# A decoder step in which the tail's memory pools wait for single tiles of the heads' memory

## The chip, the cores and the metric

The kernel runs on one core of a Trainium2 chip. The metric is device time in microseconds (us), from launch to the last output, as the median of several runs. The core has a matrix engine (PE), a vector engine (DVE), an activation engine (ACT), a general engine (POOL) that here mostly issues transfers, a sync engine (SP) that issues the other transfers, and 16 DMA engines that both issuers share. Each engine works through its own list of instructions in order; where one depends on another engine or on a transfer, it waits for a semaphore.

## The reference, cut to what matters

One inference step of one decoder layer on 512 prompt tokens and 8 sample tokens, in fp32. Two branches run side by side on the same normed input and are merged through gates; an MLP follows.

```python
h = _rmsnorm(x, norm1_g[l]) * (1.0 + sc1) + sh1
u = h @ w_in[l].astype(F32)
qa, fa, ia, oga, xb, yb, ga, gb = _split_cols(u)
...
o, S_new = _hgrn2(q, k, v, logf, st_hg[l])            # branch a: 8 heads, matrix state
o_a = (_rmsnorm(o, hg_onorm_g[l]) * jax.nn.silu(oga)).reshape(B, L, HG_HEADS * HG_DV)
...
hseq, h_last = _rglru(xc, r, ig, lru_lambda[l], st_lru[l])   # branch b: 1024 scalar recurrences
o_b = hseq * jax.nn.gelu(yb)

merged = (jax.nn.sigmoid(ga) * (o_a @ w_branch_a[l])
          + jax.nn.sigmoid(gb) * (o_b @ w_branch_b[l]))
x = x + g1 * (merged @ w_out[l])
h2 = _rmsnorm(x, norm2_g[l]) * (1.0 + sc2) + sh2
x = x + g2 * (jnp.square(jax.nn.relu(h2 @ w_ff1[l])) @ w_ff2[l])
```

## The kernel before

All activations stand transposed, 128 features by 520 tokens to a tile (512 prompt, 8 sample). A matrix product is made of three passes: each fp32 operand is split into a rounded part (`hi`) and the rest (`lo`), ACT makes the first (a cast) and DVE the second (a subtraction), and PE adds up hi·hi, hi·lo and lo·hi. One output block of 128 features takes 8 blocks of the input, each 6 matmuls (three products, two halves of 260 tokens), all at line 151. Weights come in by SP into `wst`, 512 KB at a time, and are split at lines 112 (ACT) and 115 (DVE).

The program has these stages. A start-up (to about 54 us in the profile) norms the input. Then `run` goes through the eight heads: `head` makes a head's columns, `rg_x`, `rg_y` and `rg_scans` make the blocks of branch b between them, and after every second head `heads_prompt` and `head_prompt` do the recurrence of two heads in levels (b = 1, 2, 4 ... 64: PE products of tile `X` at lines 664 to 673, then a DVE multiplication of `X` in place at line 680). Each finished block of branch b goes to DRAM (`obT_d`, line 856), each finished head too (`oaT_d`, line 749). Eight gate blocks follow (`gate`, line 175 is their sigmoid); behind the fourth of them stand `end_recurrences` and `begin_tail`.

`begin_tail` closes the pools of the heads and of branch b (`hg`, `rg`) and opens the tail's pools over the same memory: `tail` (five tiles `t` for loads), `ab` (sixteen tiles `a`: the split inputs of branch b, two to a block, and later the merged ones), `abb` (sixteen tiles `b`: the split inputs of branch a) and `misc`. `load_branches` then has POOL load the eight blocks of `obT_d` into `t` (line 882), each split into two `a` tiles by ACT (line 205) and DVE (line 206), and after them the eight of `oaT_d` (line 886, split into `b`). `load_xT` loads `xin` (line 929) on the same queue. The product with `w_branch_b` reads the `a` tiles block by block; between its matmuls stand small products of modulation rows (`mod_rows`, line 413), which read `wst` without a split.

A pool opened over memory that another pool has used makes its tiles wait for what was there. The pools `rg` and `hg` are opened with `reuse_waits="tile"`, so that a tile waits for the users of the very tiles it lies over. The tail's pools are opened without it: the first tile of each waits for everything that its pool's region held.

Instructions are put in order by a scheduler that runs a timing model over the whole program; `with self.urgent()` and `with self.together()` raise the priority of what stands under them. Each engine's order is then fixed.

Of the kernel before, what the change touches and what calls it, by code (L numbers as in the profile page):

```python
# [6 lines left out]
F32 = mybir.dt.float32  # L7
# [4 lines left out]
OP = mybir.AluOpType  # L12
# [6 lines left out]
T = L + NB  # L19
# [57 lines left out]
class Kernel:  # L77
# [383 lines left out]
    def norm_samples(self):  # L461
        nc = self.nc
        j = self.pmm.tile([128, 2, 512], F32, name="mm").rearrange("p a b -> p (a b)")
        nc.vector.tensor_tensor(j[:NB], self.xsn, self.xsn, OP.mult)
        nc.vector.tensor_reduce(self.ss1[:NB, NC:NC + 1], j[:NB], mybir.AxisListType.X, OP.add)

# [69 lines left out]
    def head_f(self, h, ps):  # L536

        nc = self.nc
        f = self.slot(self.ma, "ma")
        X = self.hg.tile([128, 3, T], F32, name="X", bufs=4)  # L540
        k = X[:, 1]
        with self.urgent():
            self.sigmoid(self.two(f), ps)
            self.sigmoid(self.two(k), ps, scale=-1.0)
        nc.vector.tensor_scalar(f, f, self.lb1[:, h:h + 1], self.lbf[:, h:h + 1], OP.mult, OP.add)
        nc.vector.tensor_scalar(k, k, self.lb1[:, h:h + 1], None, OP.mult)
        return f, X

# [7 lines left out]
    def head(self, h, first=None):  # L556
        nc = self.nc
        kf, kq, kv, kg = ([x] for x in self.head_cols(h))
        st = self.head_load(h)
        f, X = self.head_f(h, first[0] if first else self.gemm(kf, self.h)[:, :, :HALF])  # L560
        q = self.head_q(X[:, 2], first[1] if first else self.gemm(kq, self.h)[:, :, :HALF])
        og = self.slot(self.hg, "e")
# [22 lines left out]
        fkq = self.fkq[h % 4]  # L585
        for j, t in enumerate((f, X[:, 1], q)):
            nc.vector.tensor_copy(fkq[:, j, :NB], t[:, L:])  # L587
# [48 lines left out]
    def heads_prompt(self, hs):  # L636
        nc = self.nc
        two = [self.opened[h] for h in hs]
        tbs = [x[0][:, :L] for x in two]
        Xs = [x[1] for x in two]  # L640
        Ts = [self.hg.tile([128, 508], F32, name="tb", bufs=2) for _ in hs]
        to = 0
        a32 = self.hg.tile([128, 2, NC, 32], F32, name="a32", bufs=1)
        at = self.at

        def view(t, first_q, first_k, step, n, b):

            return bass.AP(tensor=t.tensor, offset=t.offset + first_q,
                           ap=[t.ap[0], [T + first_k - first_q, 2], [step, n], [1, b]])

        heads = lambda m, *shape: m[:, None].to_broadcast([128, 2, *shape])
        b = 1
        while b < C:
            n = L // (2 * b)
            p = self.pps.tile([128, 512], F32, name="ps")
            with self.together():
                for e, X in enumerate(Xs):
                    Q, K = X[:, 0], X[:, 1]
                    for c in range(NC):
                        if b == 1:  # L660
                            for j in range(4):
                                s, o = c * C + 32 * j, 256 * e + 64 * c
                                o = p[32 * j:32 * j + 32, o:o + 64].rearrange("p (x t) -> p x t", x=2)
                                nc.tensor.matmul(o, K[:, s:s + 32], X[:, 0::2, s:s + 32], start=True, stop=True)
                        elif b <= 32:
                            for j in range(0, 128, 32 if b < 32 else 64):
                                s, o = c * C + j, 128 * e + 32 * c
                                d = s if b < 32 else s + 32
                                nc.tensor.matmul(p[j:j + 32, o:o + 32], K[:, s:s + 32], Q[:, d:d + 32], start=True,
                                                 stop=True)  # L670
                        else:
                            s, o = c * C, 256 * e + 64 * c
                            nc.tensor.matmul(p[:64, o:o + 64], K[:, s:s + 64], Q[:, s + 64:s + 128], start=True,
                                             stop=True)
                if b == 64:
                    po = self.heads_sample(hs)
            for X, tb in zip(Xs, tbs):
                half = view(X, b, 0, 2 * b, n, b)
                fac = bass.AP(tensor=tb.tensor, offset=tb.offset, ap=[tb.ap[0], [1, 2], [2, n], [0, b]])
                nc.vector.tensor_tensor(half, half, fac, OP.mult)  # L680
            if b == 1:
                first = p.rearrange("p (e c x t) -> p e c x t", e=2, c=NC, x=2)
                nc.vector.tensor_tensor(a32, first[:, :, :, 1], heads(self.mdiag, NC, 32), OP.mult)
                p = first[:, :, :, 0]
            if b <= 16:
                p = p if b == 1 else p[:, :256].rearrange("p (e c t) -> p e c t", e=2, c=NC)
                nc.vector.copy_predicated(a32, heads(self.masks[b], NC, 32), p)
            elif b == 32:
                for j in (0, 64):
                    nc.scalar.copy(at[j:j + 32, :, :, j + 32:j + 64],  # L690
                                   p[j:j + 32, :256].rearrange("p (e c t) -> p e c t", e=2, c=NC))
            else:
                nc.scalar.copy(at[:64, :, :, 64:], p[:64].rearrange("p (e c t) -> p e c t", e=2, c=NC))
            for e, tb in enumerate(tbs):
                t2 = tb.rearrange("p (n two) -> p n two", two=2)
                tbs[e] = Ts[e][:, to:to + n]
                nc.vector.tensor_tensor(tbs[e], t2[:, :, 0], t2[:, :, 1], OP.mult)
            to += n
            b *= 2
        for j in range(0, 128, 32):  # L700
            nc.vector.tensor_copy(at[j:j + 32, :, :, j:j + 32], a32[j:j + 32])
        for e, h in enumerate(hs):
            self.head_prompt(h, tbs[e], at[:, e])
        self.heads_sample_done(hs, po)
# [929 lines left out]
    def begin(self):  # L1634
# [3 lines left out]
        nc = self.nc = InOrder(self.tc)  # L1638
# [162 lines left out]
        nc = plain  # L1801
        self.rgp = self.open_pool("rg", 2, reuse_waits="tile")
        self.hg = self.scope.enter_context(self.tc.tile_pool(name="hg", bufs=2, reuse_waits="tile"))
        self.opened = {}
        self.fkq = [self.hg.tile([128, 3, 32], F32, name=f"fkq{n}", bufs=1) for n in range(4)]
        self.at = self.hg.tile([128, 2, NC, C], F32, name="at", bufs=1)
        for t in (*self.fkq, self.at):
# [19 lines left out]
    def begin_tail(self):  # L1827
        self.close_pool()
        tc = self.tc
        self.misc = self.ctx.enter_context(tc.tile_pool(name="misc", bufs=1, side="right"))  # L1830
        self.right = ExitStack()
        self.abb = self.right.enter_context(tc.tile_pool(name="abb", bufs=16, side="right"))
        self.tail = self.open_pool("tail", 2)
        self.ab = self.scope.enter_context(tc.tile_pool(name="ab", bufs=16))
        self.load_branches()

    def begin_strassen(self):
# [36 lines left out]
```

## Time and profile before

| what | value |
|---|---|
| median of 3 runs | 1029.59 us (1029.26 to 1031.78) |
| profiled execution: its time | 1029.2 us |
| profiled execution: span from first to last instruction | 1027.4 us |
| PE busy | 997.1 us, 97% of the span |
| DVE, ACT, POOL busy | 677.3, 514.0, 123.8 us |
| mean clock granted to PE | 0.997 of full speed |

The span is 1.8 us shorter than that execution's time. PE sets the pace: what can be gained or lost is the time in which PE stands still, or is made to, so a wait of another engine counts only if PE ends up waiting for it. In the rows of the profile, "[2.02 <-ACT a L205]" behind an instruction says that its engine was idle 2.02 us before it, and that the idle time ended with ACT's instruction of line 205 that writes tile `a`. A matmul of plain fp32 operands counts twice (x8 are four instructions).

### The profile page before, as it was taken

What the parts mean: (1) busy time and instruction counts of PE and PEld (TensorE: products, weight loads), DVE (VectorE), ACT (ScalarE), POOL (GpSimd) and SP (SyncE); (2) the same over time, 40 slices, a digit from 0 to 9 for tenths busy, and PEclk for the clock granted to TensorE, in tenths of its full rate; (3) what the DMA queues carried; (4) which work ended last, traced back from release to release, by engine and by line L of the source; (5) the groups of instructions that cost most, each with busy time, mean ns of one, the idle gap of its engine ahead of it and who ended that gap; (6) DMA issues with size and microseconds to landing.
All of it is one profiled execution on the core that took longest, in us unless ns stands there. A gap on an engine that the chain in (4) does not pass through costs nothing. (4 is left out here: it accounts for less than half of the span.)

```text
span 1027.4 us, 23569 instructions
## 1 busy us (share of the span) xinstructions
PE 997.1 (97%) x9756; PEld 965.4 (94%) x9756; DVE 677.3 (66%) x1428; ACT 514.0 (50%) x964; POOL 123.8 (12%) x229
## 2 busy tenths in 40 slices
PE   4999999999999999989999999999999999999997
PEld 2899899999999999969999999999999999999997
DVE  6785868687596867355233347677776776777685
ACT  4555644644574563342122235466556655656663
POOL 3210000000000001011000001011321231232150
PEclk9999999999999999999999999999999999999999
DMA  9673353444334435268555568322672484274242
GB/s 324 218 206 110 98 157 103 136 130 133 101 105 147 116 115 166 90 230 265 165 162 167 164 182 242 91 83 63 134 183 74 93 181 118 52 160 98 63 83 84
DMA packets 201822, 143.67 MB, mean 140 GB/s; under 512 B 6767, under 2 KB 189703, under 8 KB 201707
## 3 DMA queue, kind: packets, MB, share of 16 engines
q1 hardware_dynamic: 191090, 128.08, 41.7%
q0 software_dynamic: 10608, 14.05, 6.9%
q8 instruction: 76, 1.25, 0.5%
q14 instruction: 32, 0.25, 0.1%
q10 hardware_dynamic: 16, 0.03, 0.0%
HBM read 123.61 MB, written 11.26 MB: 131 GB/s over the span
## 5 line engine op out<-in xcount | busy, mean ns | idle before, releaser
L151 PE MATMUL mm<-h,whi 128*128 128x260 f32 (+1 forms) x2944 | 489.5, 285 | 0.1
L151 PEld LDWEIGHTS mm<-h,whi 128*128 128x128 f32 x2944 | 409.1, 188 | 4.5 <-ACT whi L112 3.3
L151 PE MATMUL mm<-h,wlo 128*128 128x260 f32 x1472 | 301.9, 284 | 0.0
L115 DVE TENSOR_TENSOR wlo<-wst,whi 128x1024 fp32r<-128x1024 f32 x164 | 200.0, 1221 | 121.5 <-ACT whi L112 120.4
L112 ACT CAST whi<-wst 128x1024 fp32r<-128x1024 f32 x164 | 171.9, 1049 | 206.7 <-PE mm L151 178.8
L151 PEld LDWEIGHTS mm<-h,wlo 128*128 128x128 f32 x1472 | 230.1, 189 | 0.6 <-issue 0.4
L151 PE MATMUL mm<-a,whi 128*128 128x260 f32 x512 | 84.3, 285 | 2.0 <-ACT a L205 2.0
L151 PEld LDWEIGHTS mm<-a,whi 128*128 128x128 f32 x512 | 70.4, 188 | 4.6 <-ACT a L205 2.5
L151 PE MATMUL mm<-a,wlo 128*128 128x260 f32 x256 | 52.3, 284 | 0.0
L882 POOL DMA_DIRECT2D t<-obT_d x8 | 4.4, 550 | 384.5 <-PE ps L623 343.1
L1275 DVE TENSOR_TENSOR f<-f 128x260 f32<-128x260 f32 x64 | 27.3, 427 | 27.6 <-ACT f L1270 26.9
L1264 ACT ACTIVATE ft<-ft,fsh 128x512 f32<-128x512 f32 (+2 forms) x36 | 24.0, 675 | 36.1 <-DVE ft L1261 36.1
L151 PE MATMUL mm<-b,whi 128*128 128x260 f32 x256 | 41.1, 282 | 0.0
L1267 POOL TENSOR_TENSOR ft<-ft,fsh 128x8 f32<-128x8 f32 x28 | 18.3, 655 | 187.1 <-DVE ft L1261 187.1
L151 PEld LDWEIGHTS mm<-a,wlo 128*128 128x128 f32 x256 | 39.6, 188 | 0.0
L151 PEld LDWEIGHTS mm<-b,whi 128*128 128x128 f32 x256 | 35.0, 188 | 0.0
L1309 POOL DMA_DIRECT2D ma<-snap x28 | 27.7, 1003 | 34.5 <-issue 25.8
L680 DVE TENSOR_TENSOR X<-X,tb 128x512 f32<-128x512 f32 x48 | 31.7, 681 | 0.0
L1291 POOL DMA_DIRECT2D ma<-snap x28 | 26.0, 927 | 41.1 <-DMA ma<-snap 29.2
L1270 ACT ACTIVATE f<-ft 128x520 f32<-128x520 f32 (+1 forms) x36 | 20.8, 587 | 15.0 <-POOL ft L1268 13.0
L596 ACT ACTIVATE st<-st,fkq 128x128 f32<-128x128 f32 x64 | 19.6, 389 | 14.1 <-DVE fkq L587 7.3
L597 DVE SCALAR_TENSOR_TENSOR st<-vb,fkq,st 128x128 f32<-128x128 f32 x64 | 17.5, 345 | 13.5 <-DMA vb<-vd 13.5
(571 smaller groups left out, 1876.0 us busy)
## 6 DMA issues: line engine op xcount, KB each, us to landing
wst<-in_w_in_dram SPq DMA_DIRECT2D x64, 512.0 KB, 4.2
wst<-in_w_mod_dram SPq DMA_DIRECT2D x32, 512.0 KB, 4.7
wst<-in_w_ff_dram SPq DMA_DIRECT2D x64, 256.0 KB, 3.5
wst<-in_w_ff_dram SPq DMA_DIRECT2D x32, 512.0 KB, 5.0
wm<-in_w_mod_dram SPq DMA_DIRECT2D x16, 512.0 KB, 10.6
st<-in_state_hgrn_dram SPq DMA_DIRECT2D x8, 512.0 KB, 4.6
vb<-vd SPq DMA_DIRECT2D x8, 512.0 KB, 3.8
out_dram<-st SPq DMA_DIRECT2D x8, 512.0 KB
```

The source lines that it names most:

```text
L112: ins = self.nc.scalar.copy(hi, st)
L115: self.nc.vector.tensor_tensor(lo, st, hi.bitcast(F32), OP.subtract)
L151: self.last_product = self.nc.tensor.matmul(ps[s][:, :c.stop - c.start], x, y[:, c], start=first and n == 0, stop=last and n == 2)
L596: nc.scalar.activation(st[:, b], st[:, b], AF.Copy, scale=fkq[:, 0, b:b + 1])
L597: nc.vector.scalar_tensor_tensor(st[:, b], vb[:, b], fkq[:, 1, b:b + 1], st[:, b], OP.mult, OP.add)
L680: nc.vector.tensor_tensor(half, half, fac, OP.mult)
L1264: nc.scalar.activation(t[:, :p], t[:, :p], AF.Relu, bias=sh[:, 0:1])
L1267: eng.tensor_tensor(t[:, p:], t[:, p:], sh[:, 1:9], OP.add)
L1270: nc.scalar.activation(f, self.two(self.ft)[:, a:a + n], AF.Square)
L1275: self.nc.vector.tensor_tensor(f[:, n], f[:, a], f[:, b], op)
L1291: nc.gpsimd.dma_start(x[1][:, b], v[:, :n], accum_op=OP.add)
L1309: nc.gpsimd.dma_start(x[t][:, a], s[p], accum_op=OP.add)
```

## The change

Three edits. The four `X` tiles (one per head, reused after four heads) are no longer four buffers of one name in `hg` but four tiles of their own, allocated first in that pool, so that they lie at its low end and the other tiles of the heads move up. The DVE multiplication at line 680 gets the raised priority of `together`. And the four pools of the tail are opened with `reuse_waits="tile"`.

```diff
@@ head_f
-        X = self.hg.tile([128, 3, T], F32, name="X", bufs=4)
+        X = self.X[h % 4]
@@ heads_prompt
-                nc.vector.tensor_tensor(half, half, fac, OP.mult)
+                with self.together():
+                    nc.vector.tensor_tensor(half, half, fac, OP.mult)
@@ begin
         self.opened = {}
+        self.X = [self.hg.tile([128, 3, T], F32, name=f"X{n}", bufs=1) for n in range(4)]
         self.fkq = [self.hg.tile([128, 3, 32], F32, name=f"fkq{n}", bufs=1) for n in range(4)]
@@ begin_tail
         tc = self.tc
-        self.misc = self.ctx.enter_context(tc.tile_pool(name="misc", bufs=1, side="right"))
+        pool = lambda name, bufs, **kw: tc.tile_pool(name=name, bufs=bufs, reuse_waits="tile", **kw)
+        self.misc = self.ctx.enter_context(pool("misc", 1, side="right"))
         self.right = ExitStack()
-        self.abb = self.right.enter_context(tc.tile_pool(name="abb", bufs=16, side="right"))
-        self.tail = self.open_pool("tail", 2)
-        self.ab = self.scope.enter_context(tc.tile_pool(name="ab", bufs=16))
+        self.abb = self.right.enter_context(pool("abb", 16, side="right"))
+        self.tail = self.open_pool("tail", 2, reuse_waits="tile")
+        self.ab = self.scope.enter_context(pool("ab", 16))
         self.load_branches()
```

Line numbers behind the first edits move up by one to three (line 882 is 883 afterwards). With buffer numbers left out, the five engines have the same instructions in the same order in both programs: the raised priority at line 680 and the new place of `X` move nothing. What differs is the semaphores that some instructions wait for (each name in the brackets is a counter: DMAHW of SP's transfers, DMASW of POOL's, the others of an engine).

ACT, at the place where the inputs of branch b are cast; before:

```order
L755 ACTIVATE sq_5988<-os 128x64 [waits DVE_49]
L205 CAST a<-t 128x520 [waits DMAHW2_49,DMAHW3_49,DMAHW1_49,DMAHW4_49,DMASW5_49,DMAHW7_49,PE_49,Activation_49]
L205 CAST a<-t 128x520 [waits DMASW6_49]
L205 CAST a<-t 128x520 [waits DMASW7_49]
L205 CAST a<-t 128x520 [waits DMASW0_49]
L205 CAST a<-t 128x520 [waits DMASW1_49]
L112 CAST whi<-wst 128x1024 [waits DMAHW4_49]
```

and now:

```order
L756 ACTIVATE sq_5984<-os 128x64 [waits DVE_49]
L205 CAST a<-t 128x520 [waits DMASW5_49]
L205 CAST a<-t 128x520 [waits DMASW6_49]
L205 CAST a<-t 128x520 [waits DMASW7_49]
L205 CAST a<-t 128x520 [waits DMAHW7_49,DMASW0_49]
L205 CAST a<-t 128x520 [waits DMAHW1_49,DMASW1_49]
L112 CAST whi<-wst 128x1024 [waits DMAHW4_49]
```

The first cast has lost its waits for five transfers of the heads (the last store of a head to `oaT_d` among them), for PE and for ACT itself, and keeps the one for its own load. The fourth and fifth have gained a wait for an earlier store to `obT_d`. The first subtraction at line 206 loses the same waits on DVE.

POOL, at the loads of those inputs; before:

```order
L882 DMA t<-obT_d 128x520 [waits DMASW7_49,DMASW6_49,DMAHW0_49,DMASW5_49,DMAHW1_49,DMASW3_49,DMAHW2_49,DMASW2_49,DMAHW3_49,DMASW1_49,DMAHW4_49,DMASW0_49,DMAHW5_49,DVE_49,DMAHW6_49,PE_49,DMAHW7_49,Activation_49,Pool_49]
L882 DMA t<-obT_d 128x520 x4
L929 DMA xin<-in_x_prompt_dram 128x4x128 x2
L882 DMA t<-obT_d 128x520 [waits DMASW5_49,DMASW4_49,DVE_49]
L882 DMA t<-obT_d 128x520 [waits DMASW6_49,DVE_49]
L882 DMA t<-obT_d 128x520 [waits DMASW7_49,DVE_49]
```

and now:

```order
L883 DMA t<-obT_d 128x520 [waits DMAHW2_49,DMAHW3_49,DMAHW1_49,DMAHW4_49,DMAHW0_49,DMAHW6_49,DMASW5_49,DMAHW7_49,DVE_49,PE_49]
L883 DMA t<-obT_d 128x520 [waits DMASW6_49,DMASW1_49,DMASW7_49,DMASW0_49,DVE_49]
L883 DMA t<-obT_d 128x520 [waits DMAHW1_49]
L883 DMA t<-obT_d 128x520 [waits DMAHW3_49,PE_49]
L883 DMA t<-obT_d 128x520 [waits DMAHW5_49]
L930 DMA xin<-in_x_prompt_dram 128x4x128 [waits DMAHW0_49,DMASW2_49]
L930 DMA xin<-in_x_prompt_dram 128x4x128 [waits DMASW3_49,DVE_49]
L883 DMA t<-obT_d 128x520 [waits DMASW5_49,DMAHW7_49,DMASW4_49,DVE_49]
L883 DMA t<-obT_d 128x520 [waits DMAHW7_49,DMASW6_49,DVE_49]
L883 DMA t<-obT_d 128x520 [waits DMAHW1_49,DMASW7_49,DVE_49]
```

What the first load waited for all at once is now spread over the loads. The counts behind the names say which instruction is meant: the first load's count on PE is the 89th of the 96 matmuls of line 787, and the second load's count on DVE is the last multiplication of line 835. The last three loads wait, as before, for the subtractions at line 206 of the first three blocks, which free their `t` tiles. On PE one instruction differs, the first matmul that reads an `a` tile: it loses its waits for transfers and keeps that for the cast.

## The prediction

> **What bounds the kernel now.** The first view is the busy time of each engine, the second the list of PE's waits; the third is the timeline of each engine around the change.
>
> ```profile
> PE 997.1 (97%) x9756; PEld 965.4 (94%) x9756; DVE 677.3 (66%) x1428; ACT 514.0 (50%) x964; POOL 123.8 (12%) x229
> ...
> PE ps L669 <- DVE X L680: 3.4, 5, 0.9
> ...
> PE mm L151 <- ACT a L205: 2.0, 1, 2.0
> PE pt L746 <- ACT g L742: 1.7, 1, 1.7
> ...
> PE pt L632 <- DVE e L748: 0.8, 1, 0.8
> ```
>
> PE is busy 97% of the span, so an edit that takes away no matmul can win only what PE waits. Of its waits (sum, times, longest), four lie where the change could reach: 3.4 us in five pieces behind the multiplication at line 680, 2.0 us in one piece behind the cast of an `a` tile, and 1.7 and 0.8 us in the last head's own chain. All else on that list is the start-up, and single pieces of 0.7 us or less. Here is PE around the single piece:
>
> ```profile
> 444.57 3.50 PE L413 MATMUL pt<-wst,cT 128*32 128x256 f32 x30 [0.27 <-DVE os L634]
> 448.00 0.50 PE L757 MATMUL ps<-sq,ones_r 128*128 128x64 f32 x2
> ...
> 449.13 0.73 PE L151 MATMUL mm<-a,whi 128*128 128x260 f32 x4
> ...
> 452.89 0.62 PE L413 MATMUL pt<-wst,cT 128*32 128x256 f32 x2
> 455.53 0.51 PE L151 MATMUL mm<-a,whi 128*128 128x260 f32 x2 [2.02 <-ACT a L205]
> 455.97 0.63 PE L413 MATMUL pt<-wst,cT 128*32 128x256 f32 x6
> ```
>
> PE goes through five blocks of branch b from 449.13 on without a pause, is done at 453.51, and stands until 455.53 for the sixth. Why the sixth is late is read backwards from ACT, DVE and POOL:
>
> ```profile
> 444.55 0.26 ACT L755 ACTIVATE sq<-os 128x64 f32<-128x64 f32 x1 [2.40 <-DVE os L634]
> 446.17 2.73 ACT L205 CAST a<-t 128x520 fp32r<-128x520 f32 x5 [1.36 <-DMA oaT_d<-e]
> ...
> 454.86 0.62 ACT L205 CAST a<-t 128x520 fp32r<-128x520 f32 x1 [4.02 <-DMA t<-obT_d]
> 455.65 0.63 ACT L205 CAST a<-t 128x520 fp32r<-128x520 f32 x1 [0.17 <-DMA t<-obT_d]
> 456.48 0.63 ACT L205 CAST a<-t 128x520 fp32r<-128x520 f32 x1 [0.20 <-DMA t<-obT_d]
> 446.82 3.14 DVE L206 TENSOR_TENSOR a<-t,a 128x520 fp32r<-128x520 f32 x5 [2.31 <-ACT a L205]
> 402.30 0.60 POOL L882 DMA_DIRECT2D t<-obT_d  x1 [343.10 <-PE ps L623]
> 403.10 2.13 POOL L882 DMA_DIRECT2D t<-obT_d  x4 [0.20 <-issue]
> 405.23 1.51 POOL L929 DMA_DIRECT2D xin<-in_x_prompt_dram  x2
> 447.82 1.76 POOL L882 DMA_DIRECT2D t<-obT_d  x3 [41.09 <-DVE a L206]
> ```
>
> The first five blocks have been in `t` since about 410 us, but ACT may not cast them before the last head's store (`oaT_d<-e`) has landed: it idles 1.36 us and starts at 446.17. DVE follows, the first `t` tile is free, and only then, at 447.82, POOL loads the sixth block. It lands seven microseconds later, and its cast ends at 455.48.
>
> **The change part by part.** *The X tiles and the priority.* The order on all five engines is unchanged, so the 3.4 us behind line 680 stay where they are; the waits that `X`, `fkq`, `at` and the first state loads gain or lose around 53 to 60 us belong to start-up transfers and matmuls that end before those instructions are reached. Cost 0; if one of them bound, PE would show a wait between 60 and 70 us, where it has none.
>
> *The cast.* Its wait for the store goes. It still stands behind the activation of line 755, which needs the last head's `os` and which no edit touches; that one ends at 444.55 + 0.26 = 444.81. The five casts of the row above start 0.55 us apart at 0.62 us each, so a cast starts some 0.08 us before the one ahead of it ends: 444.73 now against 446.17, **1.44 us earlier**. PE gains nothing from this directly, because it reaches the first block at 449.13 in any case, held by the 30 passes of line 413 and by line 757. What gains is the sixth block, 1.44 us earlier on every step: the subtraction, the free tile, the load's issue (446.4), and, if the load takes as long, the cast (454.0). PE's wait shrinks from 2.02 to about 0.6 us.
>
> *How long the load takes* is the open cost.
>
> ```profile
> t<-obT_d POOLq DMA_DIRECT2D x1, 260.0 KB, 4.4
> t<-obT_d POOLq DMA_DIRECT2D x1, 260.0 KB, 7.0
> 445.57 0.38 SPq L103 DMA_DIRECT2D wst<-in_w_branch_b_dram  x1
> 446.42 1.31 SPq L101 DMA_DIRECT2D wst<-in_w_mod_dram  x2
> 444.75:448.00 3.25, 3.25 (x30) 1.28 (x22) 1.18 (x2) 1.89 (x5) 0.18 (x1) 0.50 0.44 141
> 448.25:453.50 5.25, 5.25 (x38) 4.15 (x38) 3.64 (x9) 1.70 (x3) 2.29 (x5) 1.00 0.98 308
> ```
>
> The same 260 KB land 4.4 us after their issue at 402.30 and 7.0 us after it at 447.82. The difference is SP's: it has issued three weight blocks of 512 KB just ahead, and the DMA engines (the last two columns are their busy share and GB/s) are full, 0.98 at 308 GB/s, from 448 on, and less than half busy before. From 446.4 on the load has one or two such blocks ahead of it in place of three. The ends: it takes 4.4 us and PE does not wait at all (gain 2.02), or it still lands at 454.86 (gain 0). I take the shift of 1.44 with the 7.0 us kept, nearest to the row with the same neighbours.
>
> The Trainium skill (DMA: Bandwidth & Descriptors, section "Queues, rings and completion order") has each DMA engine take turns between the queues of SP and POOL, packet by packet. By that the load would get about half of 308 GB/s wherever it stands: an estimate of 1.7 us for 266 KB and some 2 us of fixed time, under 4 us. The row of 7.0 us speaks against so even a split here; with it the wait would go wholly, which is the upper end above.
>
> *The blocks behind.* The seventh and eighth have room of their own: their casts follow 0.8 us apart (455.65, 456.48), while PE in between does products of the next output block. PE's next wait could be for the modulation rows issued at 446.42, if the `t` loads now pass them: 260 KB at 308 GB/s is 0.86 us, and the first such product stands directly before the sixth block (452.89).
>
> *The early loads.* Released tile by tile, the first load leaves after the 89th matmul of line 787, the next four and `xin` after the last multiplication of line 835 and a scan, instead of at 402.30.
>
> ```profile
> L787 PE MATMUL pb<-xcs,bdhlru_wa x16: 281/284/374, 255.3 to 366.6; 128*128 128x260 f32 x16
> 366.35 0.49 PE L787 MATMUL pb<-xcs,bdhlru_wa 128*128 128x260 f32 x2
> 388.50 0.69 DVE L835 TENSOR_TENSOR gate<-gate,xc 128x520 f32<-128x520 f32 x1
> 389.85 1.28 DVE L680 TENSOR_TENSOR X<-X,tb 128x512 f32<-128x512 f32 x2
> 391.45 0.76 PE L669 MATMUL ps<-X 128*32 128x32 f32 x64
> 366.50:367.00 0.50, 0.50 (x6) 0.50 (x6) 0.44 (x1) 0.50 (x2) 0.00 (x0) 1.00 0.00 0
> 389.00:393.00 4.00, 4.00 (x92) 3.82 (x92) 4.00 (x10) 2.08 (x3) 0.00 (x0) 1.00 0.23 67
> ```
>
> That is about 367 for one load, with the DMA engines idle, and 389.2 to 393 for the rest, with them 23% busy. Nobody reads these tiles before 444, so their being early is worth nothing. Their price is bounded below by 0, as the DMA engines have room. Above, it is DVE, which has no idle time in 389 to 393 and makes the `X` that PE's products wait for: if DVE stood still for each issue in that stretch (4 + 2 at the 0.54 us that POOL shows for one), 3.2 us. Against that stand the subtractions that ran in the very time of POOL's issues:
>
> ```profile
> L206 DVE TENSOR_TENSOR a<-t,a x16: 692/694/702, 446.8 to 611.7; 128x520 fp32r<-128x520 f32 x16
> L882 POOL DMA_DIRECT2D t<-obT_d x8: 539/542/599, 402.3 to 449.0; - x8
> ```
>
> All sixteen took 692 to 702 ns, the five beside POOL's issues too. I take 0. The Trainium skill (SBUF — State Buffer, section "SBUF: two separate sides") warns of this very change: POOL writes the descriptors of its transfers through a port pair that some DVE operations lock, and either side blocks the other. By it the loads at 389 would be slow, which is harmless here, or DVE would be held. The trace shows neither.
>
> *The sum.* 1029.2 (this execution: span 1027.4 and 1.8 around it) less 1.44 gives 1027.8. The median of the runs is 0.39 above that execution, so 1028.2.
>
> **The rivals.**
>
> *No wait is left.* The load lands in under 6.4 us and the 2.02 us go entirely: 1029.59 − 2.02 = 1027.6. For it: emptier DMA engines at 446.4. Against: two of SP's three blocks leave within a microsecond of it.
>
> *Another wait takes its place.* The transfers are the limit, not their issue: from 448 on the engines are full, and whichever of the `t` loads and modulation rows goes first, the other is late. PE stops at 452.89 for rows or at the sixth block at the same time as now: no gain, 1029.6. For it: the 0.98; against: some microseconds before 448 with room, which the earlier issue uses.
>
> *DVE is held at 389.* The one mechanism that ends slower: 3.2 us of issues on POOL stop DVE while it works without a pause on the last two heads. PE's product at 391.45 follows the end of DVE's `X` at 391.13 by 0.3 us, so it is late by 2.9, and less 1.44 that is +1.4: 1031.0. It decides as soon as DVE loses more than 0.3 + 1.44 us there. Against: the 692 to 702 ns.
>
> *The clock.* After the idle pieces of the last head's chain, PE ran at half its clock from 444.75 to 448.00 (the 0.50 in the window above). Were that stretch absent in another execution, half of 3.25 us, 1.6, would come on top: 1026.6. The change doesn't touch what leads to it, so this is chance between executions, in both kernels.
>
> *The change does nothing* is true of the `X` tiles and the priority, and is part of the sum.
>
> **How the numbers follow.** Forecast 0.50; no wait left 0.18; another wait in its place 0.17; DVE held 0.09; the clock 0.06. The forecast is that of the likeliest, 1028.2. The range runs from the clock's 1026.6 to 1030.2: the no-gain case and 0.6 of scatter, as the runs of before lie up to 2 us above their median; the slower case lies outside. A measurement of this kernel can tell about 0.3%, 3.1 us, from no change: none of the cases is further off than 3.0, so faster by more is 0.05 (clock and full gain together), slower by more 0.03 (DVE held longer, or something unseen), within it 0.92.
>
> **What would show it.** ACT's first cast of an `a` tile starts 0.2 us behind line 755 in place of 1.6; POOL's sixth load follows 1.4 us earlier relative to that, and PE's wait for a cast is 0 to 0.8 us. POOL's first load no longer waits for line 623 but leaves 35 us before it, four follow behind line 835. PE's five waits behind line 680 stay at 3.4 us together, within some tenths. Wrong would be: a new PE wait for `wst` between 452 and 460; more than 4 us behind line 680, or DVE operations near 390 longer than their kind; or a cast that still waits for something else of the heads.

## The result, and the profile after

The changed kernel takes 1030.64 us (median of 12 runs, 1029.19 to 1035.83); the kernel before, measured again beside it, takes 1031.11 us (12 runs, 1028.84 to 1033.85). The ratio over all these runs (not of the two medians) is 1.0003 with a 95% interval of 0.9988 to 1.0018: no difference that can be told. The predicted range, 1026.6 to 1030.2 us around 1028.2, does not hold the time. The profiled execution took 1030.22 us, its span is 1028.4 us, against 1027.4 before.

PE's busy time (first view) and the waits of PE (second) in the changed kernel:

```profile
PE 997.9 (97%) x9756; PEld 965.4 (94%) x9756; DVE 678.3 (66%) x1428; ACT 513.9 (50%) x964; POOL 123.8 (12%) x229
```

```profile
PE ps L669 <- DVE X L681: 4.1, 5, 1.1
...
PE pt L413 <- DMA wst<-in_w_mod_dram: 2.0, 1, 2.0
PE pt L747 <- ACT g L743: 1.7, 1, 1.7
...
PE pt L632 <- DVE e L749: 0.8, 1, 0.8
```

The 2.0 us for the cast of an `a` tile are gone from the list, and 2.0 us for modulation rows (`wst`) stand in their place. The waits behind the multiplication of `X` grew from 3.4 to 4.1. The timeline of PE, ACT, POOL and SP at the place of the change:

```profile
444.86 0.65 PE L632 MATMUL pt<-ident,sev 128*128 128x128 f32 x4 [0.79 <-DVE e L749]
445.78 3.48 PE L413 MATMUL pt<-wst,cT 128*32 128x256 f32 x30 [0.27 <-DVE os L634]
...
456.06 0.62 PE L413 MATMUL pt<-wst,cT 128*32 128x256 f32 x2 [1.98 <-DMA wst<-in_w_mod_dram]
456.61 0.50 PE L151 MATMUL mm<-a,whi 128*128 128x260 f32 x2
445.76 0.26 ACT L756 ACTIVATE sq<-os 128x64 f32<-128x64 f32 x1 [2.40 <-DVE os L634]
445.92 2.72 ACT L205 CAST a<-t 128x520 fp32r<-128x520 f32 x5
...
454.72 0.62 ACT L205 CAST a<-t 128x520 fp32r<-128x520 f32 x1 [2.56 <-DMA t<-obT_d]
367.60 0.60 POOL L883 DMA_DIRECT2D t<-obT_d  x1 [311.50 <-PE pb L788]
390.74 2.14 POOL L883 DMA_DIRECT2D t<-obT_d  x4 [22.54 <-DVE gate L836]
447.56 1.76 POOL L883 DMA_DIRECT2D t<-obT_d  x3 [52.59 <-DVE a L206]
446.92 0.38 SPq L103 DMA_DIRECT2D wst<-in_w_branch_b_dram  x1
447.77 1.31 SPq L101 DMA_DIRECT2D wst<-in_w_mod_dram  x2
```

The casts do what was foretold: the first starts 0.16 us behind line 756's activation, where it was 1.62 us, and the sixth `t` load leaves 1.80 us behind that activation instead of 3.27. It lands 7.16 us later (447.56 to 454.72), as before (7.04). Its cast ends at 455.34, but PE is not waiting for it: two modulation products stand in front of the sixth block, and their rows, issued at 447.77, are there only at 456.06, 8.3 us later. Before, they were issued at 446.42 and read at 452.89 without a wait, so within 6.5 us. The sixth block starts 11.75 us behind the transposes of line 632 (456.61 less 444.86); before it was 11.88 (455.53 less 443.65). So 0.13 us came of 1.44.

When a transfer has landed can be read from the trace even where nobody waits for it: its semaphore is raised sixteen times, and the last time is the landing. In each of the seven profiles in which PE stood still for rows, it went on 0.04 to 0.05 us behind that mark. By it the rows took 8.24 us in this profile and 6.38 in the kernel before, where they landed at 452.80 and PE read them at 452.89: there they had 0.09 us to spare.

Upstream the profiled execution lost time. DVE's wait for `vb`, which the last pair of heads brings through DRAM (`vs` to `vd` to `vb`), and what PE then waits for:

```profile
377.22 2.19 DVE L597 SCALAR_TENSOR_TENSOR st<-vb,fkq,st 128x128 f32<-128x128 f32 x8 [2.49 <-DMA vb<-vd]
```

```profile
366.81 0.49 PE L788 MATMUL pb<-xcs,bdhlru_wa 128*128 128x260 f32 x2
382.58 1.04 PE L669 MATMUL ps<-X 128*32 128x32 f32 x64 [0.23 <-DVE a L688]
388.27 0.46 PE L669 MATMUL ps<-X 128*32 128x32 f32 x32 [0.96 <-DVE X L681]
```

In the kernel before, the wait for `vb` was 1.69 us and PE's at this place 0.43. From the matmul at 366.81 to the last passes of line 669 (397.43) it now takes 30.62 us, before 29.82 (366.35 to 396.17): 0.80 us lost, in the very stretch where the first early load (367.60) now runs. Whether it is the cause is what some of the runs below are about.

### The profile page after: what moved, and what is told of

It is laid out like the page before. It is cut to its first block, busy times and chain, and to the rows that moved or that the text cites. A ratio compares the mean times of both kernels' runs of the same rounds, so it can differ in the third digit from the quotient of the medians.

```text
span 1028.4 us, 23561 instructions
## 1 busy us (share of the span) xinstructions
PE 997.9 (97%) x9756; PEld 965.4 (94%) x9756; DVE 678.3 (66%) x1428; ACT 513.9 (50%) x964; POOL 123.8 (12%) x229
## 5 line engine op out<-in xcount | busy, mean ns | idle before, releaser
L151 PE MATMUL mm<-b,wlo 128*128 128x260 f32 x128 | 25.9, 284 | 0.0
```

The source lines that it names most:

```text
L151: self.last_product = self.nc.tensor.matmul(ps[s][:, :c.stop - c.start], x, y[:, c], start=first and n == 0, stop=last and n == 2)
```

## The experiments

The theory after the result: in the transition from heads to branch b the transfers are the limit, since `t` loads and modulation rows share the DMA engines, and whichever goes first makes the other late; and the first early load slows the last round trip by 0.8 us. The rivals are scatter, a part of the X layout, and rows that are late by themselves.

### The casts alone

```diff
-        self.tail = self.open_pool("tail", 2, reuse_waits="tile")
+        self.tail = self.open_pool("tail", 2)
```

> The changed kernel, but the pool of the t tiles waits for all of the heads' memory as before; the casts keep their tile-wise waits. Theory (the transfers limit the transition, and the first early load costs the last heads a slower round trip through memory): the five t loads leave at about 402 again; DVE's first wait for vb after 370 is back from 2.5 to about 1.7 us and PE's waits behind line 681 from 4.1 to about 3.4 together; in the transition nothing changes against the changed kernel: no wait for a cast of a, and one stop of about 2.0 us for modulation rows; time about 0.8 us under the changed kernel's, which is within what a comparison can tell from no change. Rival A (the 0.8 us is scatter between executions or comes from the X tiles or the priority): 4.1 and 2.5 stay as they are. Rival B (the casts gain only because the loads were early): PE waits 2.0 us for the cast of a again.

Measured: 1029.95 us, ratio to the kernel before 0.9998 (0.9982 to 1.0014). The profile of this run, PE's waits, PE's stop and POOL's first load:

```profile
PE ps L669 <- DVE X L681: 3.2, 5, 0.8
```

```profile
455.22 0.62 PE L413 MATMUL pt<-wst,cT 128*32 128x256 f32 x2 [2.02 <-DMA wst<-in_w_mod_dram]
402.70 2.73 POOL L883 DMA_DIRECT2D t<-obT_d  x5 [346.50 <-PE ps L623]
```

The wait for `vb` was 1.47 us. All that the theory said came, and the stop for rows is there without early first loads. (1.47 us for `vb` is within what the rival, scatter, allows too.)

### The loads alone

```diff
-        pool = lambda name, bufs, **kw: tc.tile_pool(name=name, bufs=bufs, reuse_waits="tile", **kw)
+        pool = lambda name, bufs, **kw: tc.tile_pool(name=name, bufs=bufs, **kw)
```

> The changed kernel, but only the pool of the t tiles waits tile by tile; the pools of the a and b tiles wait as before, so the loads are early and the casts are not. Theory: ACT's first cast waits for the last head's store again and starts about 1.6 us behind line 756; PE waits about 2.0 us for the sixth block's cast and not for rows; the early loads' price stays: vb's wait 2.5 us, PE's waits behind line 681 about 4.1 together. Time about as the changed kernel's or 0.1 us above it. Rival A (scatter): 3.4 and 1.7 as in the kernel before, with the first load still at 367. Rival B (early loads also help the transition): the stop for the cast is under 1.5 us.

Measured: 1031.04 us, ratio 1.0014 (0.9999 to 1.0028). The wait for `vb` was 3.73 us, PE's behind line 681 3.9 and 0.7 more behind line 688: upstream as the theory said, and more. The transition was a miss. PE's stop and the sixth cast:

```profile
456.52 0.62 PE L413 MATMUL pt<-wst,cT 128*32 128x256 f32 x2 [1.09 <-DMA wst<-in_w_mod_dram]
456.17 0.62 ACT L205 CAST a<-t 128x520 fp32r<-128x520 f32 x1 [3.07 <-DMA t<-obT_d]
```

The first cast did wait for the store again (1.08 us), but the sixth load, issued at 450.06, landed in 6.1 us, and PE stopped 1.1 us for the rows (issued at 448.67), not 2.0 for the cast. Which of the two is late is not fixed by the casts' start alone. The rows landed 7.80 us behind their issue here, although the `t` load left 1.39 us behind them, as in the kernel before (1.40), where they took 6.38:

```profile
448.67 1.74 SPq L101 DMA_DIRECT2D wst<-in_w_mod_dram  x2
450.06 1.76 POOL L883 DMA_DIRECT2D t<-obT_d  x3 [53.84 <-DVE a L206]
```

So rows can be late by as much without a `t` load close to them.

### Modulation rows later, in the changed kernel

```diff
-            if m <= TAIL or m % 2:
+            if m > 1:
                 mod_step()
```

> The changed kernel with the modulation steps of branch b's first two output blocks done behind its fifth and seventh; the same work, other places. Theory (the transfers limit; rows and t loads compete): PE no longer stops for rows between 450 and 462, as nothing there reads any; SP's places are filled with later weight blocks instead, so the sixth block still lands about 7 us behind its issue and PE may wait for its cast, now the first thing late, 0.5 to 1.6 us; so 0.4 to 1.5 us under the changed kernel. Rival A (PE is held by something else at this place and the wait for rows only names it): a stop of 2 us stays. Rival B (the rows were the only late thing): no stop at all, 2.0 us under.

Measured: 1029.37 us, ratio 0.9994 (0.9982 to 1.0007). No stop at all between 447 and 462: the second rival. The sixth load was issued at 448.28 and landed in 5.9 us:

```profile
454.16 0.63 ACT L205 CAST a<-t 128x520 fp32r<-128x520 f32 x1 [1.71 <-DMA t<-obT_d]
```

PE was through the fifth block at 454.74, 9.2 us behind line 632, and went on without a pause. Its first product then cannot have been one of the sixth block, whose cast ended only at 454.79, so the new order has put another there; in the old order that cast would have held PE for about 0.1 us. With the rows gone nothing else is late by more. The 2.0 us under the changed kernel that this rival named did not come: the two ratios to the kernel before differ by 0.0009, 0.9 us, which their intervals do not tell from none.

### Eight loads before the transition

```diff
-            t = self.slot(self.tail, "t")
+            t = self.slot(self.tail, "t") if n < 5 else self.more.tile([128, T], F32, name=f"t{n}")
             nc.gpsimd.dma_start(t, self.obT_d[n])
...
+    def load_heads(self, s):
+        nc = self.nc
         for h in range(H):
             t = self.slot(self.tail, "t")
+            nc.gpsimd.tensor_copy(t[:, :1], s[:, :1])
             nc.gpsimd.dma_start(t[:, :L], self.oaT_d[h])
...
+            if m == 1:
+                steps.append(([], lambda: self.load_heads(gb[1])))
...
+        self.more = self.right.enter_context(pool("more", 1, side="right"))
```

> The changed kernel with room for all eight t loads of branch b before the transition (three tiles in a pool of their own), and branch a's eight loads issued only after branch b's second output block (each behind a copy of one column on POOL that reads that block). So 3 x 260 KB leave the transition and nothing comes in their place. Theory (the transfers limit): the modulation rows land in under 6 us instead of 8.3 and PE's stop for them falls from 2.0 to under 0.5 us; no wait for a cast; gain 1.5 to 2.0 us in the transition; the early loads' 0.8 us behind line 681 stays or grows a little. Rival A (rows are late by the time of their issue, 447.8, not by the t loads beside them): they still land at about 8 us and the stop stays 1.5 to 2.0. Rival B (bandwidth comes back elsewhere): branch a's later loads make a new wait for wst of over 0.5 us between 465 and 500.

Measured: 1028.64 us, ratio 0.9988 (0.9974 to 1.0002). No stop for rows, none for a cast, and no wait of PE between 447 and 520. The scheduler read the rows some 1.1 us later here, inside the sixth block in place of ahead of it, so part of the vanished stop is that. They were issued at 448.94 and landed at 454.82, in 5.88 us; in their old place, which PE passed at 454.49, the stop would have been about 0.4 us. The last rival finds nothing.

### The first load four times

```diff
-            nc.gpsimd.dma_start(t, self.obT_d[n])
+            for _ in range(1 if n else 4):
+                nc.gpsimd.dma_start(t, self.obT_d[n])
```

> The changed kernel with its first early t load issued four times in a row into the same tile (each behind the landing of the one before), so that POOL's 260 KB transfers run beside all of the last head pair's round trip vs to vd to vb, about 367.6 to 380. So far DVE's wait for vb near 377 was 1.7 and 1.5 us without the early load, and 2.5, 3.7, 1.5 and 2.8 with it; one head pair earlier, where all kernels are alike, it was 1.7 to 4.0. Theory (the load beside the round trip makes it slower, by a varying amount): with four of them the wait for vb is 3.5 us or more, and PE's waits behind line 681 and 688 near 387 grow by 1.5 us or more against the kernel before. Rival (scatter of this round trip, load or none): 1.5 to 2.8, as without it.

Measured: 1030.84 us, ratio 1.0001 (0.9989 to 1.0014). The run misses its aim: three of the four went out only at 393.57, 399.55 and 403.48, so it is one more run with a single early load; its wait for `vb` was 1.46 us, as without. A second try puts all four first by order:

> The changed kernel with its first early t load issued four times in a row, each behind the landing of the one before, now with an order on POOL that puts all four ahead of the other loads (in the first try three of them went out only behind 393 us). So POOL's transfers of 260 KB run beside the whole round trip vs to vd to vb of the last head pair, about 367 to 380. DVE's wait for vb there was so far 1.7, 1.5, 2.8 and 1.4 us without an early load, and 2.5, 3.7, 1.5, 2.8, 1.5 and 2.8 with one. Theory A (the load delays the round trip): 3.5 us or more with four. Theory B (scatter of the round trip): 1.4 to 2.8, as without.

Measured: 1031.14 us (8 runs), ratio 1.0006 (0.9989 to 1.0022). POOL issued the four at 369.31, 372.72, 376.00 and 380.42; DVE's wait:

```profile
379.36 2.19 DVE L597 SCALAR_TENSOR_TENSOR st<-vb,fkq,st 128x128 f32<-128x128 f32 x8 [2.90 <-DMA vb<-vd]
```

2.9 us is under the 3.5 of theory A and a little over the 2.8 of theory B. It stays open.

### The pools alone, in the kernel before

The edit leaves out the `X` tiles and the priority of line 680, and keeps `begin_tail`.

> The kernel before with tile-wise waits in the four pools of the tail and nothing else: no X tiles in their place, no priority of line 680. Theory (the X tiles and the priority do nothing; the order is the same): as the changed kernel, first load at 367 to 369, first cast 0.2 us behind the activation of line 755, a stop of about 2.0 us for rows and none for the cast. Rival (the X tiles are what lets the loads or casts leave early): the first load at a later time, above 380, or the cast behind the last head's store again.

Measured: 1029.82 us, ratio 1.0001 (0.9986 to 1.0015). The first load left at 367.33, the first cast started 0.16 us behind line 755: neither the loads nor the casts need the `X` tiles or the priority. But there was no stop for rows, which the theory had put at 2.0 us. PE was slower: the 30 passes of line 413 took 3.63 us, and PE reached the first block of branch b 6.5 us behind line 632 instead of 5.4. And the rows were earlier: they landed 6.25 us behind their issue (448.28 to 454.53), not 8.24. In the changed kernel's profile PE came to the rows 6.31 us behind their issue; at that pace they would have been there too. Thus the slower PE alone is not the reason.

### Modulation rows later, in the kernel before

The edit of the third run, made to the kernel before.

> The kernel before with the modulation steps of branch b's first two output blocks done behind its fifth and seventh, as was done to the changed kernel (where the stop of 2.0 us went). Theory (either late thing alone stops PE; both must go): the first five casts wait for the store as before, POOL's sixth load leaves at about 447.8 and lands 5.9 us later as in the other kernel with later rows; the sixth block is then read 0.6 us earlier than before since no rows stand ahead of it, so PE stops 0.5 to 1.5 us for the cast of a. Rival A (rows alone were the limit in both kernels): no stop. Rival B (only the time of issue counts, 7.0 us landing): a stop of over 2 us.

Measured: 1030.02 us, ratio 1.0000 (0.9986 to 1.0014). PE around the stop:

```profile
445.15 1.93 PE L413 MATMUL pt<-wst,cT 128*32 128x256 f32 x30 [0.27 <-DVE os L634]
...
455.66 0.84 PE L151 MATMUL mm<-a,whi 128*128 128x260 f32 x4 [3.52 <-ACT a L205]
```

3.5 us for the cast of `a`: more than the theory's 0.5 to 1.5, and where rival B put it (over 2 us), though the load did not take that rival's 7.0 us. The load took 6.6 us (448.43 to 454.99), and PE was 1.6 us ahead, as it ran those 30 passes at full clock. So with late casts the `t` load is what PE waits for, and taking the rows away won nothing that the ratio shows. The wait for `vb` was 2.76 us, without any early load.

### The version that the runs point to

Eight loads before the transition, but the first five from 402 on as in the kernel before:

```diff
-        self.tail = self.open_pool("tail", 2, reuse_waits="tile")
+        self.tail = self.open_pool("tail", 2)
```

> The version that the runs point to: all eight t loads before the transition and branch a's after it, as in the run with eight loads, but the first five t loads leave at 402 as in the kernel before (their pool waits for all of the heads' memory), so nothing runs beside the last round trip. Theory: no stop for rows and none for a cast between 449 and 460 (2.0 us gained there), DVE's wait for vb 1.4 to 1.8 us, PE's waits behind line 681 3.2 to 3.5; about 2 us or 0.2% under the kernel before, so about 1028 where that one has 1030.1. Rival (what is won is given back by a wait in branch a, whose loads come later): a wait of over 0.5 us between 465 and 520.

Measured: 1028.68 us, ratio 0.9988 (0.9977 to 0.9998); and once more, timed beside the changed kernel:

> The best version once more (eight t loads before the transition, five of them from 402 on, branch a's loads after it), beside the changed kernel. Theory: no stop between 449 and 460 whatever the clock, and 1.5 to 2.5 us under the changed kernel; with the half clock absent in an execution another 1.6 us. Rival: the difference of the first measurement was scatter between jobs, and the two lie within 0.5 us.

Measured: 1028.10 us, ratio 0.9984 (0.9971 to 0.9998), where the changed kernel had 1029.87 in the same comparison: 1.8 us, as the theory said. No stop in the first run; in the second, with the 30 passes at full clock, PE stopped 1.12 us for rows (issued at 445.93, there at 453.64). The theory said none whatever the clock; so the rows can take 7.7 us without a `t` load beside them, and the `t` loads are at most a part of what delays them. The 1.6 us more that a full clock was to give did not come to the end either (transitions of 68.32 and 68.00 us in the table below).

### Both kernels again

> The kernel before itself once more, for the scatter of its stages. Theory: a stop for the cast of a of 2.0 us if the 30 passes of line 413 take 3.5 us, and of 2.6 to 3.6 us if they take 1.9 us at full clock, since the sixth block's landing is set by the transfers and not by PE; wait for vb near 376 between 1.4 and 2.8. Rival: the stop is 2.0 us whatever the clock.

> The changed kernel itself once more, for the scatter of its stages and, timed beside the next kernel, for their difference. Theory (the modulation rows' landing about 8 us behind their issue is what PE waits for at the sixth block; the clock ahead of it is chance): a stop for rows of 2.0 us if the 30 passes of line 413 run at half the clock (3.5 us), of 2.6 us if they run at full clock (1.9 us), none or under 1 us if PE is slower still; never a wait for a cast of a. Rival (it is the t load): the stop's name or its size changes without such a link.

Measured: the kernel before 1030.42 us (8 runs; ratio to itself 1.0008, 0.9992 to 1.0025), the changed one 1029.87 us (0.9998, 0.9986 to 1.0011). The wait for `vb` in the kernel before, 1.28, lies a little below the 1.4 to 2.8 that was expected. PE in the kernel before, this time:

```profile
443.12 1.93 PE L413 MATMUL pt<-wst,cT 128*32 128x256 f32 x30 [0.27 <-DVE os L634]
...
450.22 0.62 PE L413 MATMUL pt<-wst,cT 128*32 128x256 f32 x2 [0.35 <-DMA wst<-in_w_mod_dram]
453.75 0.51 PE L151 MATMUL mm<-a,whi 128*128 128x260 f32 x2 [2.91 <-ACT a L205]
454.19 1.08 PE L413 MATMUL pt<-wst,cT 128*32 128x256 f32 x6
```

and in the changed kernel:

```profile
445.90 3.63 PE L413 MATMUL pt<-wst,cT 128*32 128x256 f32 x30 [0.27 <-DVE os L634]
449.47 0.69 PE L758 MATMUL ps<-sq,ones_r 128*128 128x64 f32 x2
450.09 1.06 PE L413 MATMUL pt<-wst,cT 128*32 128x256 f32 x2
...
454.99 0.62 PE L413 MATMUL pt<-wst,cT 128*32 128x256 f32 x2
```

In the kernel before, the link of the theory holds: at full clock (1.93 us for the 30 passes) the stops are 0.35 and 2.91 us, 3.26 together in place of 2.02. In the changed kernel there is no stop, and here the theory's ground, rows that land about 8 us behind their issue, is gone. Their issue and the `t` load's stand as in the first profile:

```profile
447.68 1.76 POOL L883 DMA_DIRECT2D t<-obT_d  x3 [53.10 <-DVE a L206]
447.90 1.18 SPq L101 DMA_DIRECT2D wst<-in_w_mod_dram  x2
```

The `t` load is 0.22 us ahead of the rows (0.21 in the first profile), yet the rows landed in 5.47 us and not in 8.24. PE came to them 7.1 us behind their issue, later than the 6.31 of the first profile, but at 6.31 they would have been there as well. The DMA engines moved more in this execution; from 450 to 454 us, the first profile of the changed kernel and then this one (the last three columns: granted clock, DMA share, GB/s):

```profile
450.00:454.00 4.00, 4.00 (x33) 3.76 (x32) 1.78 (x5) 1.05 (x1) 0.53 (x1) 1.00 0.96 320
450.00:454.00 4.00, 4.00 (x28) 3.09 (x28) 1.84 (x6) 1.68 (x2) 0.59 (x2) 0.87 1.04 390
```

Why 320 GB/s in one execution and 390 in the other is not known.

### All profiles side by side

Each row is one profiled execution. "Upstream" runs from the matmul of line 787 (788) at about 366 to the last passes of line 669; "30 passes" is the row of line 413 behind line 632; "rows land in" runs from the issue of the rows that PE reads at the sixth block to their landing; "transition" runs from the last transposes of line 632 to the first product of branch a (513.43 in the kernel before, 514.53 in the changed one).

| run | first load at | wait for vb | upstream | 30 passes | rows land in | stop of PE | transition |
|---|---|---|---|---|---|---|---|
| before | 402 | 1.69 | 29.82 | 3.50 | 6.38 | 2.02 cast | 69.78 |
| before again | 401 | 1.28 | 29.43 | 1.93 | 5.93 | 0.35 rows, 2.91 cast | 70.99 |
| casts alone | 403 | 1.47 | 29.60 | 3.10 | 7.91 | 2.02 rows | 70.06 |
| rows later (before) | 403 | 2.76 | 30.89 | 1.93 | moved | 3.52 cast | 71.11 |
| best version | 402 | 1.44 | 29.54 | 3.47 | 5.69 | none | 68.32 |
| best version again | 403 | 1.83 | 29.98 | 1.93 | 7.66 | 1.12 rows | 68.00 |
| changed | 368 | 2.49 | 30.62 | 3.48 | 8.24 | 1.98 rows | 69.67 |
| changed again | 367 | 2.95 | 31.09 | 3.63 | 5.47 | none | 68.94 |
| pools alone | 367 | 2.75 | 30.90 | 3.63 | 6.25 | none | 68.80 |
| loads alone | 368 | 3.73 | 31.85 | 3.23 | 7.80 | 1.09 rows | 68.82 |
| first load x4, missed | 367 | 1.46 | 29.61 | 1.93 | 8.19 | 2.61 rows | 68.96 |
| first load x4 | 369 | 2.90 | 31.29 | 3.61 | 7.55 | 1.14 rows | 69.01 |
| rows later (changed) | 369 | 1.46 | 29.60 | 3.53 | moved | none | 67.45 |
| eight loads before | 368 | 2.83 | 30.95 | 2.87 | 5.88 | none | 68.19 |

*Upstream.* Six runs without an early load lie between 29.43 and 30.89, mean 29.88; seven with one between 29.60 and 31.85, mean 30.66. That is 0.8 us more in the mean, with ranges that overlap by 1.3 us, and the run with four loads (31.29) lies within the range of one. An early load probably costs some tenths; it is not shown. The same wait one head pair earlier, near 334, where all kernels alike have no such load, lies between 1.7 and 4.0 us.

*Transition.* The nine runs that have both the last three `t` loads and the rows in their old places lie between 68.80 and 70.99. Of these, the six with early casts have a mean of 69.24, the three with late ones 69.86: 0.6 us for the early casts, about what the early loads may cost upstream, and neither is clear of the scatter. The four that take loads or rows out, with the casts early, lie between 67.45 and 68.32, and below every other run.

*Rows.* With the `t` load 0.2 us ahead to 0.6 us behind their issue, the rows landed in 5.47 to 8.24 us (six profiles); with it 1.4 to 2.1 us behind, in 5.93 to 7.80 (three); without any, in 5.69 to 7.66 (three). The ranges cover one another, so that the `t` load's place makes the rows late is not shown.

## Why the prediction was wrong, by its own steps

*X tiles and priority, 0.* Right: the pools alone bring the early loads and the early casts, and PE waits as long behind the multiplication of `X` (4.1 us) as with the whole change.

*The cast, 1.44 us earlier.* Right: 0.16 us behind line 756, and the load's issue 1.47 us earlier relative to it (1.80 against 3.27).

*How long the load takes, 7.0 us kept.* Right in the profiled execution, 7.16 us from issue to cast. Over the eleven profiles with this load in its old place it landed in 4.8 to 7.1 us. The rule that was weighed there (the Trainium skill, DMA: Bandwidth & Descriptors, "Queues, rings and completion order": an even turn between the two queues) would have given under 4 us; no run came to that.

*The blocks behind.* **This step failed.** It named the modulation rows as PE's next possible wait, put what the `t` load takes from them at 0.86 us, and left it out of the sum. It did not ask how much the rows had to spare: 0.09 us in the kernel before. In the profiled execution they landed 8.24 us behind their issue in place of 6.38, 1.86 us more, while PE and with it SP's issue of the rows were not earlier (1.99 us behind the start of the 30 passes, 447.77 less 445.78; before 1.85, 446.42 less 444.57). So PE stood 1.98 us for rows where it had stood 2.02 for the cast, and of 1.44 us 0.13 came. Both of the prediction's own signs of being wrong were there: a wait for `wst` at 456.06, and 4.1 us behind the multiplication of `X` (3.4 in the second profile). Why the rows took 1.86 us more stays open. The `t` load, moved up alone, went from 1.40 us behind their issue to 0.21 us ahead of it, but the second profile of the changed kernel has it 0.22 us ahead and rows in 5.47 us, and the loads alone have it 1.39 us behind and rows in 7.80. What is shown is that the rows' landing varies by 2.8 us between two executions of the same kernel, about twice the gain that was forecast, and that PE had no slack for it.

Clearer is the second weight block on SP's queue, which is issued close to these loads and the first two of branch a's; the changed kernel first, then the best version, transfers issued from 444 to 456 us (count, size, us to landing, of two the later):

```profile
wst<-in_w_branch_b_dram SPq DMA_DIRECT2D x2, 512.0 KB, 10.9
```

```profile
wst<-in_w_branch_b_dram SPq DMA_DIRECT2D x2, 512.0 KB, 6.2
```

With the loads in their old places it takes 7.8 to 11.5 us in nine profiles (mean 10.2), without them 6.2, 6.9 and 8.4. PE did not stop for this block in any of them. The rival "another wait takes its place", given 0.17, describes the profiled execution to about a tenth of a microsecond: the stop was to stay at the sixth block or at the rows before it, with no gain. The second profile of the changed kernel, with no stop, is as the rival "no wait is left" has it; by the two profiles either can happen. Its time, 1029.39 us, was still not below the 1029.2 of the kernel before: the transition gave 0.84 us and the stretch upstream took 1.27.

*The early loads, 0.* Wrong in its way of looking, open in its size. The bound was sought in DVE being held by POOL's issues, and DVE was not: the eight operations of line 597 take 2.19 us with and without a load. What may be slower is the neighbour on the DMA engines, the round trip of `vb`, by 0.8 us in the mean of runs that scatter by as much.

*The sum.* It stood on the first median, 1029.59 us of three runs. The kernel before then measured 1031.11, 1030.10, 1030.25 and 1029.93 us over 12 and 35 runs, so the base was 0.3 to 1.5 us low, up to as much as the gain that was foretold. Of the 2.5 us between forecast and time, 1.5 are the base of the same comparison and 1.0 the gain that did not come (1.44 less the 0.47 between the two medians, which the interval does not tell from none). From 1031.11 the same sum would have given 1029.7, and a range moved likewise would have held 1030.64: the miss of the range is in good part the base, the missing gain is the step above. The chance for "no change that can be measured", 0.92, needs no amends.

*The clock* was put down as a rival that takes 1.6 us off. It comes and goes as said (3.5 or 1.93 us for the 30 passes), in the kernel before and in versions of the changed one, but its 1.6 us hardly reach the end: the kernel before at full clock stopped 3.26 us in place of 2.02 and had a transition 1.21 us longer (70.99 against 69.78), the changed kernel with its first load four times (the missed try) stopped 2.61 where the changed one stopped 1.98, and kept 0.71 us (68.96 against 69.67).

## What to carry to other kernels

When a wait for a transfer is removed by issuing that transfer earlier, ask what its reader waits for next and how much that has to spare: the next late transfer may belong to an instruction that stands one place ahead in the same engine's list. Here the modulation rows had 0.09 us. The version that takes loads out of the crowded stretch (three of branch b's eight before it, branch a's eight behind it) is 1.2 and 1.6 us faster than the kernel before by the two ratios, with intervals that end just below 1. Moving the rows alone gave the shortest transition of all profiles (67.45 us), but a time that can't be told from that of the kernel before (0.9994, 0.9982 to 1.0007). Where a stretch is limited by transfers, a faster or slower clock in it mostly changed the length of the wait rather than the end. And one profile of each kernel told a story, of a load that delays its neighbour, that the second profile of the same kernel does not bear out.

## What the runs showed of the hardware

The stretch at half clock behind the last head's idle pieces is there in ten of fourteen profiles, with the same instructions ahead of it (the 30 passes take 2.9 to 3.6 us there, 1.93 in the other four); where it was missing and a stop of about 3 us followed (two profiles), the clock fell behind that stop. In the kernel before, run again (windows: time, length, busy time and count of PE, PEld, DVE, ACT, POOL; granted clock; DMA share; GB/s):

```profile
445.50:449.00 3.50, 3.50 (x29) 3.10 (x28) 3.15 (x6) 2.94 (x5) 2.36 (x5) 1.00 0.90 293
449.00:454.00 5.00, 1.73 (x12) 1.05 (x10) 2.05 (x6) 0.68 (x2) 0.35 (x1) 1.00 1.00 362
454.00:458.00 4.00, 4.00 (x24) 2.06 (x24) 3.73 (x15) 1.25 (x2) 1.56 (x3) 0.57 1.05 384
```

The clock is 1.00 ahead of the 2.91 us stop and 0.57 behind it, and its transition is the longest but one. The same happened behind the stop of 3.52 us; behind one of 2.61 us the clock stayed at 1.00. Three runs are too few for a bound, but they suggest that removing such a stop can be worth more than its length. The Trainium skill (TensorE: Matmul & The Clock Gate, "Part 1: The HAM clock gate (the "warmup" mystery)") tells of a free-running window of some 3.4 us over which activity is judged, so that the same kernel shows different numbers of slow matmuls from run to run. The change between 3.5 and 1.93 us for like instructions fits that; but the page lets the clock fall after an idle window, and here a stop of 2.91 us and, in ten profiles of fourteen, pieces of 1.7, 0.8 and 0.3 us had it behind them.

Transfers of the same size in the same place scatter widely: 4.8 to 7.1 us for the sixth `t` load, 5.5 to 8.2 us for the modulation rows, 1.3 to 3.7 us for the wait for `vb` near 376. One profile of each kernel could not have told a cause that is worth 0.8 us from that.
